# Seven-product tiles: a buffer of its own for the third weight piece, a norm spread over twelve tiles, and one more tile by seven products

## The chip, the cores and the metric

The kernel runs on one core of a Trainium2 chip. The core has a matrix engine (PE, whose weight loads the profile lists as PEld), a vector engine (DVE, called VectorE in words), a scalar engine (ACT, ScalarE), a general engine (POOL, GpSimd) and a queue engine (SP) that issues most of the transfers between device memory and the core's own memory. The metric is the time of one execution on the device in microseconds (us). A profile is of one such execution; its span runs from the first to the last instruction.

## The reference

One layer of a streaming encoder is computed for two request groups with the same weights: 1024 frames of a new stream and 32 frames of a running one, 1056 columns in all. The first half of the layer (input projection, three kinds of mixing heads, output projection, norm) isn't touched by the change. The second half is a gated feed-forward layer and the final norm:

```python
x = _layer_norm(ALPHA * x + (1 + g1) * mix, ln1_g, ln1_b)
h = x * (1 + sc2) + sh2
y = (jax.nn.silu(h @ w_gate) * (h @ w_up)) @ w_down
x = _layer_norm(ALPHA * x + (1 + g2) * y, ln2_g, ln2_b)
```

`D_MODEL` is 1024 and `D_FF` is 2816. Everything is in 32-bit floating point.

## The kernel before, in words

**Precision.** Each operand of a large matrix product is split in two: a rounded copy ("hi", made by ScalarE) and the difference to it ("lo", made by VectorE). A product of 128 x 128 weights with a block of columns is then three matmuls, hi by hi, hi by lo and lo by hi (`gemm`, lines 117 to 119). Weights come in through `weights` (lines 105 and 106): a load into a "raw" buffer, a cast into "whi", a subtraction into "wlo". There are three buffers of each kind (`RAW`, `WB`), each of 1056 columns, used in rotation.

**Two column groups.** Group 0 holds 512 columns, group 1 holds 544 (two cuts of 272). The feed-forward layer runs for group 0 first, then for group 1. The 2816 hidden units are 22 tiles of 128, taken in six groups of tiles (`GROUPS`: 3, 3, 4, 4, 4, 4). For each group of tiles, the gate and up products and their activation are made for each tile, and then the down projection (`down`) adds the group's share to the residual `z`. One tile of the next group is made ahead of each down projection.

**Tiles of seven products.** For group 1, the tiles from `SJ` = 4 to 20 are made by `sup`. Gate and up weights, the two halves of the 1024 rows and the two cuts of columns form a product of 2 x 2 blocks by 2 x 2 blocks, and `sup` forms it with seven block products in place of eight, by sums and differences of blocks. Each block product is four 128-row steps of three matmuls over 272 columns, 12 matmuls. A tile in the plain way (`up`) takes 96 matmuls. What `sup` needs beside its own weights:

- **Combined columns.** `sup_operand` makes the sums and differences of the column blocks once, in four steps (k = 0 to 3), into the tiles `T`. Each step loads two blocks from the buffer `dh` in device memory, does four operations on VectorE (lines 1063 to 1066), and splits two results into hi and lo (lines 1068 and 1069). For even k the landing buffers are "w2h" and "w2l", for odd k the two "c" buffers. The steps run among tiles 0, 1 and 2 of group 1.
- **Summed weight blocks.** `sums` prepares, in device memory, the block `dp[j]` for tile j: a copy of one weight block, twice, issued on SP (line 91), and then an accumulating transfer issued on POOL (line 1040). It's called once for each tile, several tiles ahead.
- **Pieces.** For each tile three loads fill raw buffers: `raw[0]` with 1024 columns of `w_gu`, `raw[1]` with the 1024 columns of `dp[j]`, `raw[2]` with 512 columns of `w_gu`. From `raw[0]` comes w1 (lines 1087 and 1088); then two additions in place (lines 1093 and 1094), the first of which reads `raw[1]`, turn it into the source of w3. From `raw[1]` comes w4, and from `raw[2]` w2, whose halves have their own buffers "w2h" and "w2l".
- **Order of products.** w1 with the first rows, w1 with the second, w3, w4, w3, w4, w2. Their results are drained by lines 1113 to 1117 and 1124 and 1125, with "uv" and "c" as places for partial results, and lines 1119 to 1128 form the activation.

**Group 0's second norm.** While group 1 runs, the final norm of group 0 is done in pieces by the generator `norm0`: for each of two halves of the columns a step for statistics (with matmuls, line 863, and lines 1167 to 1169) and eight steps, one for each 128 rows. One such step has two VectorE operations (1171, 1187), one ScalarE operation (1189) and, for every second one, a store on SP (1194). Two steps follow each tile of seven products, from tile 4 to tile 12. `issue_after` keeps a step's instructions behind the tile's last activation on the same engine.

**Order.** The order of the instructions on each engine and queue is fixed when the kernel is built, by a planner that works with its own estimates of durations; the program text gives the dependencies and the preference. On the chip each engine then runs its list in order. Names in the profile follow buffers: `wo_ah` and `wo_al` are the columns' hi and lo, `lna_ah` and `lna_al` in group 1's tiles are the combined columns `T`, `mlstm_z` is the residual of group 0, `start_dp` is the summed weight block, and "sup_g" and "sup_u" are the two sets of accumulators that the products use in turn.

In the profile tile 3 of group 1 runs from 1050 to 1062 us, the first down projection from 1062 to 1080, tiles 4 to 6 from 1080 to 1113, tiles 7 to 10 from 1132 to 1180, tiles 11 to 14 from 1204 to 1251, tiles 15 to 18 from about 1276 to 1318.

Of the kernel before, what the change touches and what calls it, by code (L numbers as in the profile page):

```python
# [7 lines left out]
F32 = mybir.dt.float32  # L8
# [7 lines left out]
P = 128  # L16
# [29 lines left out]
RAW = 3  # L46
WB = 3
FF = 22
SJ = 4
TS = 1  # L50
ALPHA = 2.0 ** 0.25
LN_EPS = 1e-5
# [13 lines left out]
def f(ap):  # L66
    return ap.bitcast(F32)


class Kernel:  # L70
# [10 lines left out]
    def t(self, pool, shape, dt=F32, tag=None, bufs=None):  # L81
        self.n += 1
        kw = {} if bufs is None else {"bufs": bufs}
        return pool.tile(shape, dt, tag=tag, name=f"{self.phase}_{tag}_{self.n}", **kw)
# [945 lines left out]
    def sums(self):  # L1030
# [5 lines left out]
        if i < FF:  # L1036
            with self.tc.issue_after(self.lastload.ins):
                self.store(self.dp[i], blocks(i)[:, 2:3].to_broadcast([P, 2, 512]))
        if SJ <= i - 1 < FF:
            self.nc.gpsimd.dma_start(self.dp[i - 1], blocks(i - 1)[:, 0:4:3], accum_op=ALU.add)  # L1040

    def sup_operand(self, ks):

        nc = self.nc
        tt = nc.vector.tensor_tensor
        if not self.T:
            self.T = [[self.t(self.ph, [P, 2176], F32R, f"{x}{i}", 1).rearrange("p (k n) -> p k n", k=4)
                       for x in ("ah", "al")] for i in (0, 256)]
        a, b = slice(0, 272), slice(272, 544)
        def load(k):  # L1050
            self.phase = "sup"
            x, y = ((self.t(self.px, [P, 544], F32, "c", 2) for _ in range(2)) if k % 2 else
                    (f(self.t(self.px, [P, 544], F32R, z, 1)) for z in ("w2h", "w2l")))
            self.load(x, self.dh[:, k])
            self.load(y, self.dh[:, k + 4])
            return x, y

        loaded = {k: load(k) for k in ks[:2]}
        yield
        for k in ks:  # L1060
            self.phase = "sup"
            x, y = loaded.pop(k)
            tt(y[:, b], y[:, b], x[:, b], ALU.subtract)
            tt(x[:, b], x[:, a], x[:, b], ALU.subtract)
            tt(x[:, a], y[:, b], x[:, a], ALU.add)
            tt(y[:, a], x[:, a], y[:, a], ALU.subtract)
            for z, (h, l) in zip((x, y), self.T):
                nc.scalar.copy(h[:, k], z)
                tt(l[:, k], z, f(h[:, k]), ALU.subtract)
            if k + 2 in ks:  # L1070
                loaded[k + 2] = load(k + 2)
            yield

    def sup(self, j, act, pool):
        self.phase = "sup"
        nc = self.nc
        tt = nc.vector.tensor_tensor
        hh, hl, T = self.hh[1], self.hl[1], self.T
        ah, al = act[j] = [self.t(pool, [P, GN[1]], F32R, x, 5) for x in ("acth", "actl")]
        raw = [self.t(self.wp, [P, 1056], F32, "raw", RAW)[:, :n] for n in (1024, 1024, 512)]  # L1080
        self.load(raw[0], self.d["w_gu"][j][:, :1024])
        self.load(raw[1], self.dp[j].rearrange("p b n -> p (b n)"))
        self.load(raw[2], self.d["w_gu"][j][:, 1536:])
        lo, hi = slice(0, 512), slice(512, 1024)

        def split(h, l, x):
            nc.scalar.copy(h, x)  # L1087
            tt(l, x, f(h), ALU.subtract)  # L1088
            return [(h[:, k * P:k * P + P], l[:, k * P:k * P + P]) for k in range(x.shape[1] // P)]

        big = lambda x: split(*(self.t(self.wp, [P, 1056], F32R, y, WB)[:, :1024] for y in ("whi", "wlo")), x)
        w1 = big(raw[0])
        tt(raw[0][:, lo], raw[0][:, lo], raw[1][:, hi], ALU.add)
        tt(raw[0][:, hi], raw[0][:, hi], raw[0][:, lo], ALU.add)
        w3 = big(raw[0])
        w4 = big(raw[1])
        w2 = split(*(self.t(self.px, [P, 544], F32R, x, 1)[:, :512] for x in ("w2h", "w2l")), raw[2])
        own = lambda t, k0: (lambda k: hh[t][:, k0 + k], lambda k: hl[t][:, k0 + k])
        com = lambda i: tuple(lambda k, t=t: t[:, k, 272 * (i % 2):272 * (i % 2) + 272] for t in T[i // 2])
        n = [0]  # L1100

        def prod(w, x):
            n[0] += 1
            ps = self.t((self.pg, self.pu)[n[0] % 2], [P, 512], F32, self.utag[n[0] % 2])[:, :272]
            self.gemm(ps, w, slice(0, P), *x)
            return ps

        a, b = slice(0, 272), slice(272, 544)
        u1 = self.t(self.p2, [P, 272], F32, "tmp", 4)
        x = self.t(self.p2, [P, 544], F32, "sil", 2)  # L1110
        uv = self.t(self.px, [P, 544], F32, "uv", 1)
        c = self.t(self.px, [P, 544], F32, "c", 2)
        nc.scalar.copy(u1, prod(w1[:4], own(0, 0)))
        tt(x[:, a], prod(w1[4:], own(0, 4)), u1, ALU.add)
        tt(uv[:, a], u1, prod(w3[:4], com(0)), ALU.subtract)
        tt(uv[:, b], prod(w4[4:], com(1)), uv[:, a], ALU.add)  # L1116
        tt(x[:, b], prod(w3[4:], own(272, 4)), uv[:, b], ALU.add)
        s = self.t(self.p2, [P, 544], F32, "sil", 2)
        nc.scalar.activation(s, x, AF.Exp, scale=-1.0)
        nc.scalar.activation(s, s, AF.Ln, bias=self.one)  # L1120
        nc.scalar.activation(s, s, AF.Exp, scale=-1.0)
        tt(s, x, s, ALU.mult)
        two = lambda y: y.rearrange("p (t n) -> p t n", t=2)
        tt(two(c), prod(w4[:4], com(3)).unsqueeze(1).to_broadcast([P, 2, 272]), two(uv), ALU.add)
        tt(c[:, a], prod(w2, com(2)), c[:, a], ALU.add)
        nc.vector.scalar_tensor_tensor(c, c, -1.0, s, ALU.mult, ALU.mult)
        nc.scalar.copy(ah, c)
        self.lastact = tt(al, c, f(ah), ALU.subtract)
# [78 lines left out]
    def run(self):  # L1207
# [14 lines left out]
        self.dh = t([P, KT, GN[1]], "dh")  # L1222
        self.dp = {j: t([P, 2, 512], f"dp{j}") for j in range(SJ, FF)}
        self.T = []
        self.scq = ()
        self.nsum = SJ
        self.dmix = [t([P, KT, GN[c]], f"dmix{c}") for c in range(2)]
# [18 lines left out]
        w2, w3 = d["w_in"], d["w_in_f"]  # L1246
# [154 lines left out]
        def norm0():  # L1401
            for a, b in LN[0]:
                yield from self.ln2(0, self.st0, a, b, "aaaaaaaa")

        norm0 = norm0()
        for g, (j0, nj) in enumerate(GROUPS):
            for j in range(j0 + (g > 0), min(j0 + nj + (g < last), FF - TS)):
                if self.nsum <= FF:
                    self.sums()
                if j >= SJ:  # L1410
                    self.sup(j, act, pa)
                    with tc.issue_after(self.lastact.ins):
                        next(norm0, None)
                        next(norm0, None)
                    continue
                for i, _ in enumerate(self.up(1, j, act, pa, MM[1])):
                    if 0 < 2 * j + i // 2 < 5 and i % 2:
                        with tc.issue_after(self.lastact.ins):
                            next(operand, None)
            if g < last:  # L1420
                st = self.ln_begin(nc.gpsimd, sum=False) if g == last - 1 else None
                self.down(1, g, act, MM[1], st)
        st.update(pivot=False, sum=True, order=(4, 5, 6, 7, 0, 1, 2, 3))

        n = nj * 256
# [123 lines left out]
```

## Time and profile before

| | us |
|---|---|
| time, median of 3 runs | 1418.04 |
| lowest and highest of them | 1415.65 and 1418.85 |
| the profiled execution | 1418.36 |
| its span | 1416.6 |
| granted clock of the matrix engine, mean over the span | 0.990 |

A row of the profile's table of groups gives line, engine, operation, names (out <- in), shape and count, then busy time and the mean duration of one in ns, then the idle time of the engine just before them and what ended it. A row of the timeline gives start and duration in us. An "x2" behind a row of the timeline means that consecutive instructions of one kind are merged, and the duration covers them all. Matmuls overlap: the records show 0.29 us for one of 272 columns, while the next one starts 0.125 us later.

### The profile page before, as it was taken

The page shows a single profiled execution, that of the slowest core. Times are in us where ns is not written, and L with a number is a line of the kernel's source. Part 1 is how long each engine was busy: PE and PEld are TensorE (multiplying, and loading weights), DVE is VectorE, ACT ScalarE, POOL GpSimd, SP SyncE. Part 2 cuts the span into 40 slices and gives each one's busy share as a digit, 9 for nine tenths or more (in the row PEclk, how much of TensorE's full clock was granted, in tenths as well). Part 3 has the DMA queues.
Part 4 walks back from the last instruction along what each step waited for, and adds up shares of the span by engine and source line. Part 5 has one row for each costly group of instructions (what it writes and reads, how often), then busy time and mean ns, then how long its engine had stood idle before and what let it go on. Part 6 is the DMA issues. An engine that isn't in the chain of part 4 may idle for free.

```text
span 1416.6 us, 28810 instructions
## 1 busy us (share of the span) xinstructions
PE 1364.1 (96%) x10945; PEld 1312.5 (93%) x10945; DVE 1041.1 (73%) x2363; ACT 657.7 (46%) x1395; POOL 255.8 (18%) x298
## 2 busy tenths in 40 slices
PE   7999999999999899999999999999999999999996
PEld 4799988999889789999999999999999999999996
DVE  5548645678679678687777765678977988878777
ACT  3313234444446464555555453335663454535354
POOL 0103200043157400000000000364610000000331
PEclk9999999999999999999999999999999999999999
DMA  9664578575754765344334422654586567542321
GB/s 359 246 216 132 172 224 238 174 229 157 224 185 147 185 206 173 99 142 148 111 112 146 90 98 86 179 172 128 177 214 182 159 176 202 155 135 92 118 98 64
DMA packets 135698, 231.97 MB, mean 164 GB/s; under 512 B 22516, under 2 KB 79484, under 8 KB 135560
## 3 DMA queue, kind: packets, MB, share of 16 engines
q1 hardware_dynamic: 130520, 220.56, 49.2%
q0 software_dynamic: 4896, 9.44, 4.4%
q8 instruction: 86, 1.41, 0.4%
q14 instruction: 52, 0.43, 0.1%
q10 hardware_dynamic: 144, 0.14, 0.0%
HBM read 196.19 MB, written 52.76 MB: 176 GB/s over the span
## 4 chain that ended last, share of the span: by engine, by line
PE 76%; DVE 9%; DMA 8%; ACT 3%; issue 2%; SPq 1%; POOL 1%; DVEq 0%; ACTq 0%; POOLq 0%
PE up_g L118 6%; PE up_g L119 5%; PE up_g L117 5%; PE dn_g L117 4%; PE dn_g L118 4%; PE dn_g L119 4%; PE tm_g L282 3%; PE tm_g L283 3%; PE tm_g L284 3%; PE fm_g L117 2%; PE fm_g L119 2%; PE fm_g L118 2%; PE fox_t L732 2%; PE wo_g L117 2%; PE wo_g L118 2%
## 5 line engine op out<-in xcount | busy, mean ns | idle before, releaser
L117 PE MATMUL up_g<-wo_ah,up_whi 128*128 128x256 f32 (+1 forms) x720 | 205.4, 286 | 3.9 <-ACT lna_tmp L964 3.3
L118 PE MATMUL up_g<-wo_al,up_whi 128*128 128x256 f32 (+1 forms) x720 | 207.4, 288 | 0.6 <-DVE wo_al L969 0.6
L119 PE MATMUL up_g<-wo_ah,up_wlo 128*128 128x256 f32 (+1 forms) x720 | 205.9, 286 | 0.0
L117 PEld LDWEIGHTS up_g<-wo_ah,up_whi 128*128 128x128 f32 x720 | 136.6, 190 | 5.4 <-ACT wo_ah L968 3.5
L118 PEld LDWEIGHTS up_g<-wo_al,up_whi 128*128 128x128 f32 x720 | 136.8, 190 | 1.6 <-DVE wo_al L969 0.8
L119 PEld LDWEIGHTS up_g<-wo_ah,up_wlo 128*128 128x128 f32 x720 | 136.8, 190 | 0.4 <-DVE up_wlo L106 0.2
L117 PE MATMUL fm_g<-start_h1h,fm_whi 128*128 128x256 f32 (+2 forms) x344 | 102.1, 302 | 8.4 <-DVE fm_qkl L367 3.6
L283 PE MATMUL tm_g<-tm_wlo,start_h1h 128*128 128x256 f32 (+1 forms) x384 | 110.1, 287 | 0.0
L284 PE MATMUL tm_g<-tm_whi,start_h1l 128*128 128x256 f32 (+1 forms) x384 | 109.8, 287 | 0.0
L282 PE MATMUL tm_g<-tm_whi,start_h1h 128*128 128x256 f32 (+1 forms) x384 | 109.2, 286 | 0.2 <-ACT tm_mixs L633 0.2
L117 PE MATMUL dn_g<-up_acth,dn_whi 128*128 128x256 f32 (+1 forms) x352 | 102.4, 291 | 0.2 <-DVE sup_uv L1116 0.2
L118 PE MATMUL fm_g<-start_h1l,fm_whi 128*128 128x256 f32 (+2 forms) x344 | 101.7, 296 | 0.0
L119 PE MATMUL fm_g<-start_h1h,fm_wlo 128*128 128x256 f32 (+2 forms) x344 | 101.1, 295 | 0.0
L118 PE MATMUL dn_g<-up_actl,dn_whi 128*128 128x256 f32 (+1 forms) x352 | 100.5, 286 | 0.0
L119 PE MATMUL dn_g<-up_acth,dn_wlo 128*128 128x256 f32 (+1 forms) x352 | 100.4, 285 | 0.0
L1087 ACT CAST sup_whi<-sup_raw 128x1024 fp32r<-128x1024 f32 x51 | 52.7, 1047 | 80.7 <-PE dn_u L118 28.1
L735 ACT CAST fox_pth<-fox_t 128x256 fp32r<-128x256 f32 (+3 forms) x144 | 51.1, 373 | 67.5 <-PE fox_t L732 63.0
L117 PEld LDWEIGHTS fm_g<-start_h1h,fm_whi 128*128 128x128 f32 x344 | 65.4, 192 | 14.0 <-DVE fm_qkl L367 4.3
L106 DVE TENSOR_TENSOR up_wlo<-up_raw,up_whi 128x1024 fp32r<-128x1024 f32 x52 | 66.2, 1273 | 16.5 <-ACT up_whi L105 15.7
L1088 DVE TENSOR_TENSOR sup_wlo<-sup_raw,sup_whi 128x1024 fp32r<-128x1024 f32 x51 | 63.1, 1244 | 17.0 <-ACT sup_whi L1087 17.0
L105 ACT CAST up_whi<-up_raw 128x1024 fp32r<-128x1024 f32 x52 | 54.5, 1047 | 45.2 <-PE up_g L118 19.7
L736 DVE TENSOR_TENSOR fox_ptl<-fox_t,fox_pth 128x256 fp32r<-128x256 f32 (+3 forms) x144 | 58.0, 417 | 23.7 <-ACT fox_pth L735 22.4
(575 smaller groups left out, 4676.9 us busy)
## 6 DMA issues: line engine op xcount, KB each, us to landing
up_raw<-w_gu SPq DMA_DIRECT2D x52, 512.0 KB
dn_raw<-w_dn SPq DMA_DIRECT2D x28, 512.0 KB
ada_late<-w_ada SPq DMA_DIRECT2D x24, 512.0 KB
wo_raw<-w_o SPq DMA_DIRECT2D x24, 512.0 KB
sup_raw<-w_gu SPq DMA_DIRECT2D x19, 512.0 KB
start_dp<-w_gu SPq DMA_DIRECT2D x18, 512.0 KB
start_dp<-w_gu POOLq DMA_DIRECT2D x18, 512.0 KB, 7.6
sup_raw<-start_dp SPq DMA_DIRECT2D x17, 512.0 KB
```

The lines of the kernel that those rows point to most:

```text
L105: nc.scalar.copy(hi[:, :w], raw[:, :w])
L106: (eng or nc.vector).tensor_tensor(lo[:, :w], raw[:, :w], f(hi[:, :w]), ALU.subtract)
L117: nc.tensor.matmul(ps, hi, xh(k), start=start and k == 0, stop=False)
L118: nc.tensor.matmul(ps, hi, xl(k), start=False, stop=False)
L119: nc.tensor.matmul(ps, lo, xh(k), start=False, stop=stop and k == n - 1)
L282: nc.tensor.matmul(ps[:, :ncol], xh, hi, start=k == 0, stop=False)
L283: nc.tensor.matmul(ps[:, :ncol], xh, lo, start=False, stop=False)
L284: nc.tensor.matmul(ps[:, :ncol], xl, hi, start=False, stop=k == 7)
L735: nc.scalar.copy(ph[:, lo:nq], ps[:, lo:nq])
L736: nc.vector.tensor_tensor(pl[:, lo:nq], ps[:, lo:nq], f(ph[:, lo:nq]), ALU.subtract)
L1087: nc.scalar.copy(h, x)
L1088: tt(l, x, f(h), ALU.subtract)
```

## The change

Three edits, all in the part where group 1's feed-forward layer runs. `SJ` goes from 4 to 3: tile 3 is made by `sup`, and the sums of weight blocks begin with tile 3. The third piece of each tile gets a buffer "w2" of its own in the pool `px` and leaves the rotation of raw buffers; to make room there, "c" has one buffer in place of two, and the loads of `sup_operand` for odd k use "c" and "uv". The steps of `norm0` no longer go two to a tile: a list gives 1, 1, 2, 2, 2, 1 steps, twice, to the twelve tiles 3 to 14.

```diff
-SJ = 4
+SJ = 3
...
-            x, y = ((self.t(self.px, [P, 544], F32, "c", 2) for _ in range(2)) if k % 2 else
+            x, y = ((self.t(self.px, [P, 544], F32, z, 1) for z in ("c", "uv")) if k % 2 else
                     (f(self.t(self.px, [P, 544], F32R, z, 1)) for z in ("w2h", "w2l")))
...
-        raw = [self.t(self.wp, [P, 1056], F32, "raw", RAW)[:, :n] for n in (1024, 1024, 512)]
+        raw = [self.t(self.wp, [P, 1056], F32, "raw", RAW)[:, :1024] for _ in range(2)]
+        raw.append(self.t(self.px, [P, 544], F32, "w2", 1)[:, :512])
         self.load(raw[0], self.d["w_gu"][j][:, :1024])
         self.load(raw[1], self.dp[j].rearrange("p b n -> p (b n)"))
         self.load(raw[2], self.d["w_gu"][j][:, 1536:])
...
         uv = self.t(self.px, [P, 544], F32, "uv", 1)
-        c = self.t(self.px, [P, 544], F32, "c", 2)
+        c = self.t(self.px, [P, 544], F32, "c", 1)
...
         norm0 = norm0()
+        turns = [1, 1, 2, 2, 2, 1] * 2
...
                     with tc.issue_after(self.lastact.ins):
-                        next(norm0, None)
-                        next(norm0, None)
+                        for _ in range(turns.pop(0) if turns else 0):
+                            next(norm0, None)
                     continue
```

## The prediction, made before the changed kernel was run

> **What bounds the kernel now.** I read the page first, then the waits of the matrix engine in the last third, then a table of windows over the stage that the change touches, then the chain of waits inside it.
>
> ```profile
> span 1416.6 us, 28810 instructions
> PE 1364.1 (96%) x10945; PEld 1312.5 (93%) x10945; DVE 1041.1 (73%) x2363; ACT 657.7 (46%) x1395; POOL 255.8 (18%) x298
> ```
>
> PE is busy for 96% of the span, so a gain must come from fewer matmuls or from the few places where PE stands still. The waits of PE from 1030 us to the end (what it waited for: total us, times, longest) are few:
>
> ```profile
> PE sup_u L117 <- ACT sup_whi L1087: 5.6, 2, 2.9
> PE sup_u L119 <- DVE sup_wlo L1088: 0.7, 1, 0.7
> ```
>
> All of it lies in the tiles of seven products ("sup" names), where a weight piece wasn't split in time: 6.3 us. The table of windows (start:end, length, busy us and instructions of PE, PEld, DVE, ACT, POOL, granted clock, DMA share, GB/s) shows what they cost in all. The first three rows are tiles 7 to 10, tiles 11 to 14, and tiles 15 to 18.
>
> ```profile
> 1132.60:1175.00 42.40, 38.76 (x291) 38.04 (x291) 35.51 (x61) 23.66 (x37) 2.07 (x2) 0.96 0.65 177
> 1204.00:1250.00 46.00, 43.23 (x328) 42.63 (x327) 36.16 (x60) 23.30 (x34) 2.07 (x2) 0.96 0.59 166
> 1275.50:1318.00 42.50, 42.50 (x340) 42.50 (x340) 36.18 (x56) 24.37 (x34) 0.00 (x0) 1.00 0.35 118
> 1170.90:1174.40 3.50, 3.49 (x16) 3.50 (x17) 3.29 (x4) 2.37 (x3) 0.00 (x0) 0.53 0.79 211
> 1242.30:1245.70 3.40, 3.40 (x17) 3.40 (x18) 3.40 (x5) 2.45 (x3) 0.00 (x0) 0.57 0.71 223
> ```
>
> Tiles 15 to 18 never wait: 340 matmuls in 42.50 us, 0.125 us each. By that rate the first two windows lose 42.40 - 291 x 0.125 = 6.0 us and 46.00 - 328 x 0.125 = 5.0 us, **11.0 us together**. 6.3 us of it is standing still. The last two rows show most of the rest: right after each long wait the granted clock is 0.53 and 0.57 for 3.4 us, in which 16 and 17 matmuls run instead of 28 and 27; that is 1.5 + 1.3 us.
>
> Why the pieces are late is in the chain of waits (start us, us, what), here from tile 8 to tile 10:
>
> ```profile
> 1134.65 3.80 DMA sup_raw<-start_dp
> ...
> 1144.18 7.49 DMA sup_raw<-start_dp
> ...
> 1155.61 1.14 DVE sup_wlo L1088
> ...
> 1156.77 5.82 DMA sup_raw<-w_gu
> ```
>
> The path runs load, adds, split, load: a load starts the moment a split frees a buffer. Three raw buffers serve three pieces of each tile, so every piece of the next tile waits for a piece of this one. From 1144.18 to 1156.77 the loop takes 12.6 us, while a tile of 84 matmuls takes 84 x 0.125 = 10.5. SP's queue shows the same:
>
> ```profile
> 1142.42 0.33 SPq L87 DMA_DIRECT2D sup_raw<-w_gu  x1
> 1144.18 0.33 SPq L87 DMA_DIRECT2D sup_raw<-start_dp  x1
> 1145.13 0.33 SPq L87 DMA_DIRECT2D sup_raw<-w_gu  x1
> 1145.51 0.92 SPq L91 DMA_DIRECT2D start_dp<-w_gu  x1
> 1153.81 0.39 SPq L1194 DMA_DIRECT2D o_yT<-mlstm_z  x1
> 1156.77 0.33 SPq L87 DMA_DIRECT2D sup_raw<-w_gu  x1
> ```
>
> The first three are tile 9's pieces. Tile 10's first piece goes out only at 1156.77 and lands 5.82 later, at 1162.6, with tile 10's first product due about a microsecond after.
>
> **The change part by part.**
>
> *Tile 3 by seven products.* It ran as 2 x 2 x 8 x 3 = 96 matmuls and will run as 84. 12 x 0.125 = **-1.5 us** on PE. It adds work elsewhere: 256 KB more loaded, one more summed weight block (a store on SP, an accumulating DMA on POOL), and more VectorE work. The neighbours:
>
> ```profile
> 1025.02 1.06 POOL L1040 DMA_DIRECT2D start_dp<-w_gu  x1 [1.82 <-DMA start_dp<-w_gu]
> 1029.04 2.39 SPq L87 DMA_DIRECT2D up_raw<-w_gu  x2
> 1034.23 0.33 SPq L87 DMA_DIRECT2D sup_w2h<-start_dh  x1
> start_dp<-w_gu POOLq DMA_DIRECT2D x18, 512.0 KB, 7.6
> ```
>
> All sums move one place, so tile 3's takes POOL's place at 1025.02 and lands about 7.6 later (the median), at 1032.6. Tile 3's load of it stands where the second load of 1029.04 ended (1031.4), so SP may stand for about 1.2 us; behind it is a load that went out at 1034.23 anyway. Cost 0.
>
> The operands of tile 3 are the closer race. Its matmuls start at 1049.96 and the third product, the first that reads the combined operands, is due 24 matmuls later, at 1053.0:
>
> ```profile
> 1049.96 0.29 PE L117 MATMUL up_g<-wo_ah,up_whi 128*128 128x272 f32 x1
> 1047.03 1.05 ACT L105 CAST up_whi<-up_raw 128x1024 fp32r<-128x1024 f32 x1 [0.76 <-PE up_g L118]
> 1048.24 1.22 DVE L106 TENSOR_TENSOR up_wlo<-up_raw,up_whi 128x1024 fp32r<-128x1024 f32 x1
> 1050.37 0.43 DVE L1019 TENSOR_TENSOR up_sil<-up_g,up_sil 128x272 f32<-128x272 f32 x1
> 1050.72 0.71 DVE L1069 TENSOR_TENSOR lna_al<-sup_c,lna_ah 128x544 fp32r<-128x544 f32 x1
> 1050.00:1062.00 12.00, 12.00 (x98) 12.00 (x98) 5.72 (x11) 5.52 (x11) 1.22 (x2) 1.00 0.63 164
> 1062.00:1080.00 18.00, 18.00 (x146) 18.00 (x145) 14.51 (x31) 4.61 (x6) 1.03 (x1) 1.00 0.75 192
> ```
>
> The last operand is made at 1051.43; two adds of 0.68 each (L1093, L1094; the row of L1093 is below) put it at 52.8. The third piece of split weight (w3) can take the cast at 1047.03; the fourth needs one more cast and one more subtraction of 1.22 after 1050, due at 1054.5. So it fits with about 0.2 us to spare on VectorE, which is idle for 6.3 us of the next 12. Bounds: 0, or everything in a row on VectorE (1.22 + 1.36 + 1.24 + 1.24, two subtractions of the last operand at 0.71, three closing operations of the tile before at about 0.44, from 1048.24) until 1056.0, which is 3.0 late, plus the 1.5 of slow clock that followed the long waits: 4.5. I take the value near the rows, **+0.5**.
>
> *The third piece's own buffer.* Two of the three ring buffers are now used per tile, so tile 10's first piece waits for tile 8's fourth-weight split (free at 1144.18, by the load that took the buffer then) and not for tile 9's; behind tile 9's third piece and one store on SP it goes at about 1146.5 instead of 1156.77. The summed piece of tile 9 goes after w3's split of tile 8 (1142.4) instead of 1144.18. The rest of the loop is load 7.49 at worst, two adds, cast, subtraction:
>
> ```profile
> L1093 DVE TENSOR_TENSOR sup_raw<-sup_raw,sup_raw 128x512 f32<-128x512 f32 x17 | 11.6, 683 | 1.6 <-DMA sup_raw<-start_dp 1.6
> L1087 ACT CAST sup_whi<-sup_raw 128x1024 fp32r<-128x1024 f32 x51 | 52.7, 1047 | 80.7 <-PE dn_u L118 28.1
> L1088 DVE TENSOR_TENSOR sup_wlo<-sup_raw,sup_whi 128x1024 fp32r<-128x1024 f32 x51 | 63.1, 1244 | 17.0 <-ACT sup_whi L1087 17.0
> ```
>
> 7.5 + 1.4 + 1.05 + 1.2 = 11.2 with the slowest load and 7.5 with the fastest (3.80), against 10.5 on PE and with a tile more of lead. The waits in tile 10 go, and so does the one in tile 14, whose first piece came the same way. **-11.0 us**; bounds 0 (VectorE or ScalarE are the limit, below) and -11.0. The new buffer's load waits for the split of the third piece before it (SP order puts a sum's store and the next first piece behind it); 1145.13 shows that it waited for just that split already. Cost 0; if it slips, the piece behind it still has 10 us of lead.
>
> *One buffer for c, uv used for loading.* c is written and last read on VectorE, the next tile's write follows in its order; uv is first written by tile 3's third product, after the operand step that reads it (1051.43). Cost 0; bound 0.7, the one wait on VectorE of that length above.
>
> *The norm over twelve tiles.* The same 18 steps, each with two VectorE operations, one on ScalarE, and a store on SP for every second one. Before tile 10's late split, the second half's statistics and a step stood in the way; they move by one tile. In tiles 11 to 13 two steps per tile stay. Steps now reach tile 14 and touch nothing that tiles 15 to 20 wait for (36.18 of 42.50 on VectorE there, and no wait). Moved stores of 0.39 each sit between loads on SP as before: 0.
>
> *What is left.* Short waits of the 0.74 kind will come up somewhere in eleven reshuffled tiles: I allow **+1.0**, between 0 and 2.1 (three of 0.7).
>
> Sum: -1.5 + 0.5 - 11.0 + 1.0 = -11.0. The profiled execution took 1418.36 us (span 1416.6 and 1.8 around it), the median is 1418.04: 1418.36 - 11.0 = 1407.4 there, **1407.0** beside the median. Its own range is 1404.5 to 1410.5.
>
> [...]
>
> **The rivals.**
>
> *Tile 3 takes more.* VectorE is behind at tile 3, a long wait with its slow clock: 4.5 instead of 0.5, 1411.0. For it: 14.51 of 18.00 on VectorE right after. Against: 6.3 us idle just before that.
>
> *One of the two long waits stays*, tile 14's, where norm steps aren't thinned: 5.0 less gained, 1412.0. For it: a norm step's activation stood ahead of the late cast, as the rows show. Against: by the reckoning for tile 10 its first piece, too, comes about a tile sooner.
>
> ```profile
> 1240.13 0.60 ACT L1189 ACTIVATE mlstm_z<-mlstm_z,start_colp 128x256 f32<-128x256 f32 x1
> 1240.63 0.64 ACT L1121 ACTIVATE sup_sil<-sup_sil 128x544 f32<-128x544 f32 x1
> 1241.18 1.98 ACT L1087 CAST sup_whi<-sup_raw 128x1024 fp32r<-128x1024 f32 x2
> ```
>
> *Slow clock without waits.* If the 2.8 us at half clock came from something other than the idle time before, they stay: 1409.8. It is within the forecast's own range.
>
> *The change doesn't do what it says*: the loads aren't issued earlier, because in SP's fixed order they stand behind one that waits, or because the order of casts is what binds. Then only the 1.5 and tile 3's 0.5 count, with +1.0 left out: 1417.0.
>
> *Slower: VectorE is the bound of the tiles, not the ring.* Place: tiles 3 and 4 and the down projection between. Tiles 7 to 10 kept it busy 35.51 of 42.40. If it is full, earlier loads give nothing (0 of 11.0), and one more such tile gives two more waits like those seen: 4.5 in tile 3 and 5.0 in tile 4. 1418.0 - 1.5 + 9.5 = 1426.0. It decides from new waits over 1.5 + 2.8 = 4.3 us. Against: tiles 15 to 18 hold 36.18 of 42.50 and lose nothing.
>
> **How the numbers follow.** Forecast with its own range 0.55 (the slow clock's case, 0.03, inside); tile 3 takes more 0.12; one long wait stays 0.12; no earlier loads 0.12; slower 0.09. Within 0.2% means 1415.2 to 1420.9, about what a measurement of this kernel can tell from no change. So faster 0.55 + 0.12 + 0.12 = 0.79, same 0.12, slower 0.09. The range runs from 1404.5 (every term at its best gives 1418.04 - 12.5 = 1405.5, and 1.0 of the spread of the runs shown, 1415.65 to 1418.85) to 1418.0, which takes in every case but the slower one.
>
> **What would show it.** Right: no wait of PE on L1087 between 1120 and 1250, granted clock 1.00 there, 84 matmuls in tile 3, first pieces issued a tile ahead on SP. Wrong in tile 3: a wait on L1069, L1088 or L1093's followers near 1053. Wrong in the ring: "sup_whi <- DMA sup_raw" still on the chain with a load that starts as a split ends. Wrong on VectorE: PE waits on L1088 with the raw piece long landed.

## The result, and the profile after

| | before | after |
|---|---|---|
| time, median of 5 runs (us) | 1417.29 | 1405.29 |
| lowest and highest of them (us) | 1415.65 and 1418.85 | 1404.46 and 1406.04 |
| the profiled execution (us) | 1418.36 | 1406.04 |
| its span (us) | 1416.6 | 1404.3 |

The change makes the kernel faster: the ratio of the times is 0.9916, with a 95% interval of 0.9904 to 0.9927. The medians differ by 12.0 us, the two spans by 12.3.

First the head of the page of the changed kernel, the same two lines as before:

```profile
span 1404.3 us, 28827 instructions
PE 1360.3 (97%) x10933; PEld 1310.1 (93%) x10933; DVE 1042.7 (74%) x2370; ACT 657.6 (47%) x1394; POOL 258.2 (18%) x299
```

There are 12 matmuls fewer, tile 3's, and yet PE is busy for only 3.8 us less, while the span is 12.3 us shorter. So most of what went was time in which PE stood still or ran at half clock (in the kernel before, the granted clock was 0.50 for 3.41 us behind each of the two long waits; last section). Next the waits of PE from 1030 us to the end in the changed kernel (what it waited for: total us, times, longest):

```profile
PE up_u L119 <- DVE up_wlo L106: 0.4, 1, 0.4
PE lnb_t L863 <- DVE sup_qs L853: 0.2, 1, 0.2
PE lnb_t L863 <- POOL sup_zs L851: 0.2, 1, 0.2
```

The 6.3 us of waits for the casts and subtractions of the seven-product tiles are gone (in the changed program those lines are 1088 and 1089). The table of windows of the changed kernel follows, with the columns of the prediction's (start:end, length, busy us and instructions of PE, PEld, DVE, ACT, POOL, granted clock, DMA share, GB/s). Its rows are tile 3, the first down projection, tiles 7 to 10, and tiles 11 to 14:

```profile
1050.80:1062.00 11.20, 11.20 (x89) 11.14 (x88) 9.43 (x17) 6.87 (x12) 1.03 (x1) 1.00 0.96 274
1062.00:1080.30 18.30, 18.30 (x146) 18.25 (x146) 16.38 (x36) 5.49 (x10) 2.05 (x2) 1.00 0.90 217
1130.50:1173.00 42.50, 42.50 (x340) 42.45 (x339) 36.75 (x60) 24.64 (x37) 1.03 (x1) 1.00 0.59 169
1197.10:1239.40 42.30, 42.30 (x339) 42.30 (x338) 37.11 (x62) 24.59 (x35) 1.03 (x1) 1.00 0.53 151
```

Tiles 7 to 14 now run as tiles 15 to 18 did before: PE without a gap, 0.125 us per matmul, the clock at 1.00. VectorE works more than before in the same windows (36.75 of 42.50, against 35.51 of 42.40), and nothing waits for it. SP's queue in the changed kernel shows what was behind the waits:

```profile
1140.59 0.32 SPq L87 DMA_DIRECT2D sup_raw<-start_dp  x1
1142.35 0.33 SPq L87 DMA_DIRECT2D sup_raw<-w_gu  x1
1143.30 0.33 SPq L87 DMA_DIRECT2D sup_w<-w_gu  x1
1143.69 0.55 SPq L91 DMA_DIRECT2D start_dp<-w_gu  x1
1150.04 0.40 SPq L1195 DMA_DIRECT2D o_yT<-mlstm_z  x1
1153.38 0.33 SPq L87 DMA_DIRECT2D sup_raw<-start_dp  x1
```

These are tile 9's summed piece, tile 10's first piece, tile 9's third piece (now in `sup_w`), a sum's store, a store of the norm, and tile 10's summed piece. Tile 10's first piece is issued at 1142.35, ahead of tile 9's third. The first matmul that needs it starts 20.2 us later:

```profile
1162.55 0.29 PE L117 MATMUL sup_u<-wo_ah,sup_whi 128*128 128x272 f32 x1
```

Before, the same matmul started at 1163.77, 7.0 us after the issue at 1156.77.

**Where the 12.3 us lie.** To compare kernels by stage I use a point that all of them pass at the same place of the work: the last statistics matmul of group 1's first norm, ahead of its feed-forward layer. Its rows, before and after (durations in ns, then the first and last start in us):

```profile
L863 PE MATMUL lna_t<-wo_qs,start_onesm x2: 392/392/392, 990.1 to 990.3; 128*128 128x272 f32 x2
```

```profile
L863 PE MATMUL lna_t<-wo_qs,start_onesm x2: 392/392/392, 991.0 to 991.2; 128*128 128x272 f32 x2
```

From there to the end it was 1416.6 - 990.3 = 426.3 us and is 1404.3 - 991.2 = 413.1: the stage is 13.2 us shorter, and 0.9 came back ahead of it. I call this length "the stage" below.

### The profile page after: what moved, and what is told of

The parts are those of the page before. It is cut to its first block, busy times and chain, and to the rows that moved or that the text cites. A ratio compares the mean times of both kernels' runs of the same rounds, so it can differ in the third digit from the quotient of the medians.

```text
span 1404.3 us, 28827 instructions
## 1 busy us (share of the span) xinstructions
PE 1360.3 (97%) x10933; PEld 1310.1 (93%) x10933; DVE 1042.7 (74%) x2370; ACT 657.6 (47%) x1394; POOL 258.2 (18%) x299
## 4 chain that ended last, share of the span: by engine, by line
PE 81%; DMA 7%; DVE 7%; ACT 2%; issue 1%; SPq 1%; POOL 1%; DVEq 0%; ACTq 0%; POOLq 0%
PE up_g L118 5%; PE up_g L119 5%; PE up_g L117 5%; PE dn_g L117 4%; PE dn_g L118 4%; PE dn_g L119 4%; PE tm_g L282 3%; PE tm_g L283 3%; PE tm_g L284 3%; PE sup_u L119 3%; PE sup_u L117 3%; PE sup_u L118 3%; PE fox_t L732 2%; PE wo_g L118 2%; PE fm_g L117 2%; PE wo_g L117 2%
## 5 line engine op out<-in xcount | busy, mean ns | idle before, releaser
L117 PE MATMUL up_g<-wo_ah,up_whi 128*128 128x256 f32 (+1 forms) x704 | 200.6, 286 | 4.1 <-ACT lna_tmp L964 3.4
L118 PE MATMUL up_g<-wo_al,up_whi 128*128 128x256 f32 (+1 forms) x704 | 202.4, 288 | 0.6 <-DVE wo_al L969 0.6
L119 PE MATMUL up_g<-wo_ah,up_wlo 128*128 128x256 f32 (+1 forms) x704 | 200.9, 286 | 0.0
L117 PEld LDWEIGHTS up_g<-wo_ah,up_whi 128*128 128x128 f32 x704 | 133.3, 190 | 5.6 <-ACT lna_tmp L964 3.5
L118 PEld LDWEIGHTS up_g<-wo_al,up_whi 128*128 128x128 f32 x704 | 133.4, 190 | 1.4 <-DVE wo_al L969 0.8
L119 PEld LDWEIGHTS up_g<-wo_ah,up_wlo 128*128 128x128 f32 x704 | 133.6, 190 | 0.4 <-DVE up_wlo L106 0.2
L1088 ACT CAST sup_whi<-sup_raw 128x1024 fp32r<-128x1024 f32 x54 | 56.0, 1048 | 91.4 <-PE dn_u L118 47.8
L1089 DVE TENSOR_TENSOR sup_wlo<-sup_raw,sup_whi 128x1024 fp32r<-128x1024 f32 x54 | 68.0, 1263 | 10.7 <-ACT sup_whi L1088 10.7
L282 PEld LDWEIGHTS tm_g<-tm_whi,start_h1h 128*128 128x128 f32 x384 | 73.5, 192 | 2.6 <-issue 1.6
L106 DVE TENSOR_TENSOR up_wlo<-up_raw,up_whi 128x1024 fp32r<-128x1024 f32 x50 | 63.3, 1265 | 16.5 <-ACT up_whi L105 16.2
```

Source lines behind the costliest of these rows:

```text
L106: (eng or nc.vector).tensor_tensor(lo[:, :w], raw[:, :w], f(hi[:, :w]), ALU.subtract)
L117: nc.tensor.matmul(ps, hi, xh(k), start=start and k == 0, stop=False)
L118: nc.tensor.matmul(ps, hi, xl(k), start=False, stop=False)
L119: nc.tensor.matmul(ps, lo, xh(k), start=False, stop=stop and k == n - 1)
L282: nc.tensor.matmul(ps[:, :ncol], xh, hi, start=k == 0, stop=False)
```

## The experiments

All ratios are to the kernel before, with 95% intervals. The stage is read from one profile of each kernel. Kernels without waits that should agree in the stage lie up to about 1.3 us apart, so smaller differences say nothing; with the long waits it is more, since a half clock that costs some 1.5 us (28 matmuls less 16, of 0.125 us each) may or may not follow a wait (last section).

| kernel | ratio | stage (us) | PE waits for splits of the seven-product tiles, 1100 us to the end (us) |
|---|---|---|---|
| before | 1 | 426.3 | 6.3 |
| the change | 0.9916 (0.9904 to 0.9927) | 413.1 | 0 |
| tile 3 alone | 0.9972 (0.9954 to 0.9990) | 421.0 | 5.0 |
| own buffer alone | 0.9951 (0.9937 to 0.9965) | 414.1 | 0 |
| spread norm alone | 0.9989 (0.9978 to 1.0001) | 423.0 | 5.6 |
| own buffer and spread norm | 0.9959 (0.9944 to 0.9973) | 414.9 | 0 |
| tile 3 and own buffer | 0.9919 (0.9901 to 0.9938) | 412.3 | 0 |
| tile 3 and spread norm | 0.9989 (0.9975 to 1.0004) | 423.7 | 6.3 |

### One part alone

My theory was that the ring of three raw buffers is the cause, and the own buffer the cure. The rivals were that the norm's steps in the way of the splits are the cause, so that spreading them is the cure, and that the sparing in tile 3 is worth more than its matmuls. The first three runs each make one part of the change alone.

```diff
-SJ = 4
+SJ = 3
```

> Tile 3 by seven products alone, ring and norm as before. Theory (the ring's short supply makes the two long waits): the waits of some 11 us stay somewhere in tiles 4 to 14, only 12 matmuls of 0.125 us go: 1.5 faster, ratio 0.999. Rival (norm crowding makes the waits): the norm now starts a tile earlier with two steps to a tile, so the waits stay too, perhaps moved: 0.999. Rival (any new order of the planner is as good as the change): the waits go here too: 0.991.

The two waits stayed, as this view of its PE waits from 1100 us on shows:

```profile
PE sup_u L117 <- ACT sup_whi L1087: 4.5, 2, 3.0
PE sup_g L117 <- ACT sup_whi L1087: 0.5, 2, 0.4
```

The stage is 5.3 us shorter, of which 1.5 are matmuls, and the ratio, 0.9972, is better than expected. I put the other part down to chance, which no second profile shows: the second long wait was 1.5 us in this execution, and the mean granted clock was 0.991, against 0.990 before. One stretch at half clock less, some 1.5 us by the matmuls in such a stretch (last section), would make up part of it, an estimate. Fewer matmuls alone don't mend the ring.

```diff
-        raw = [self.t(self.wp, [P, 1056], F32, "raw", RAW)[:, :n] for n in (1024, 1024, 512)]
+        raw = [self.t(self.wp, [P, 1056], F32, "raw", RAW)[:, :1024] for _ in range(2)]
+        raw.append(self.t(self.px, [P, 544], F32, "w2", 1)[:, :512])
```

(with the two edits to "c" and "uv" that make room for it)

> The third piece's own buffer alone (with one c buffer and uv as landing place), tiles of seven products from tile 4 and two norm steps to a tile as before. Theory (ring): both long waits go, about 11 us, ratio 0.992, first pieces are issued a tile earlier on SP. Rival (norm crowding): the waits stay, ratio 1.000. A split result, one wait gone and one kept, gives 0.996.

No wait for a split is left, and the stage is 12.2 us shorter. That is the whole gain of the stage but for tile 3's. The time as a whole gained less, 0.9951: ahead of the stage something was lost, which is followed up below.

```diff
+        turns = [1, 1, 2, 2, 2, 1] * 2
...
-                        next(norm0, None)
-                        next(norm0, None)
+                        for _ in range(turns.pop(0) if turns else 0):
+                            next(norm0, None)
```

> The norm spread over twelve tiles (4 to 15) alone, ring and first tile as before. Theory (ring): the waits stay, ratio 0.999 to 1.000, with the chain still running load, split, load. Rival (norm crowding): both long waits go, ratio 0.992.

The waits stayed at 5.6 us:

```profile
PE sup_u L117 <- ACT sup_whi L1087: 5.6, 2, 4.3
```

The time is within 0.2% of the kernel before. Spreading the norm is not the cure.

### One part left out

Leaving out one part of the whole change tests the same from the other side. The change without tile 3:

> The change without tile 3: third piece's own buffer and the spread norm. Theory and the norm rival alike: 11 us gained, ratio 0.9925, 1.5 us slower than the whole change. If tile 3's earlier start were itself what loosened the stage, this would stay near 1.000.

The stage is 414.9, 1.8 us longer than with tile 3 and within scatter of the own buffer alone (414.1). The ratio, 0.9959, misses the 0.9925 expected; as with the own buffer alone, something was lost ahead of the stage. The change without the spread norm:

> The whole change without the spread norm (two steps to a tile, from tile 3). Theory (the own buffer alone removes the waits): no wait of PE on a split between 1040 and 1330, from the last statistics of group 1's first norm to the end about 413 us, as with the whole change, ratio 0.992. Rival (the spread norm is needed once tile 3 is a tile of seven products too): a wait of 1 us or more in tiles 3 to 10, ratio above 0.995.

It is as fast as the whole change (0.9919 against 0.9916), and its stage is 412.3. The spread norm is worth nothing that can be measured here. The change without the own buffer:

> The whole change without the own buffer: tile 3 by seven products and the spread norm, three pieces in the ring. Theory: waits on the split of w3 stay (one of 3 to 4 us and one of 1 to 1.5, as with each of the two alone), some 5 to 7 us of the 11 are left, ratio 0.996. Rival (both easings add up): no wait, ratio 0.992.

All the waits are back, and the ratio is 0.9989, with an interval that holds 1. I had expected that half of the gain would be left (0.996):

```profile
PE sup_u L117 <- ACT sup_whi L1087: 5.8, 2, 3.1
PE sup_u L119 <- DVE sup_wlo L1088: 0.5, 1, 0.5
```

So the own buffer carries the change. In the eight kernels of the table the waits are gone wherever it is in, and there wherever it is out.

### Is the norm a cause at all?

Spreading it did nothing, but that leaves open whether the waits need it. The next kernel is the one before with group 0's second norm left out, so that the rows of the output that belong to group 0 aren't written.

```diff
-                        next(norm0, None)
-                        next(norm0, None)
+                        pass
```

> The kernel before with group 0's second norm left out altogether (its output rows stay unwritten), ring of three for three pieces. Theory (the ring's short supply is the cause, the norm's instructions only add to it): waits on the splits of 1 us or more stay. Rival (VectorE and ScalarE are too full with the norm): no wait at all in tiles 4 to 14, 11 us gained plus about 0.7 for its statistics, ratio 0.991.

The ratio is 0.9933 (0.9911 to 0.9954), the stage 415.4. PE waits for splits in three short waits, 1.4 us together and none longer than 0.5. Neither expectation came true: the theory wanted waits of 1 us or more, the rival none at all.

```profile
PE sup_g L117 <- ACT sup_whi L1087: 0.9, 2, 0.4
PE sup_u L117 <- ACT sup_whi L1087: 0.5, 1, 0.5
```

The loop of load and split is still in its chain of waits, with loads that start as a split ends:

```profile
1137.46 1.06 ACT sup_whi L1087
1138.54 1.24 DVE sup_wlo L1088
1139.79 6.55 DMA sup_raw<-w_gu
1146.42 1.06 ACT sup_whi L1087
```

So the long waits have two causes together: the ring leaves hardly any slack, and the norm's instructions on the same engines use up more than there is. Taking either away ends the long waits. Moving the norm by a tile or two doesn't take it away.

### Lead, or the third piece out of the way?

The own buffer does two things: it gives the other two pieces a third buffer to share, so that they are loaded a tile ahead, and it takes the third piece's split out of the ring. This kernel is the whole change, with one of the three ring buffers held by an unused tile until tile 16. The third piece keeps its own buffer; the lead is taken away.

```diff
+        keep = self.t(self.wp, [P, 1056], F32, "raw", RAW)
+        nc.vector.memset(keep[:, :1], 0.0)
...
+                        if j == 16:
+                            nc.vector.tensor_copy(keep[:, 1:2], keep[:, :1])
```

> The whole change, but one of the three ring buffers is held by an unused tile from group 1's first tile to tile 16, so that the third piece keeps its own buffer and the other two pieces have one buffer each, as the three pieces had before. Theory (the lead that the freed ring buffer gives is what counts): the waits come back, of the size of before or more, since the plain tiles and the down projections have two buffers as well: 10 us or more slower than the whole change, ratio 1.000 or above. Rival (getting the third piece out of the others' way is enough): ratio 0.992 to 0.994.

All of the gain is gone: the ratio is 1.0011 (0.9997 to 1.0025), the stage 422.8, and the waits are back:

```profile
PE sup_u L117 <- ACT sup_whi L1088: 5.4, 2, 3.0
PE sup_u L118 <- DVE lna_al L1069: 0.3, 1, 0.3
```

In SP's queue tile 10's first piece goes out 8.3 us before its first matmul (at 1160.85), against 20.2 with the change and 7.0 before:

```profile
1152.57 0.33 SPq L87 DMA_DIRECT2D sup_raw<-w_gu  x1
```

The lead is what counts, and not that the third piece is out of the way. The down projections in between had two buffers as well, so this kernel doesn't tell the tiles' share of the lead from theirs.

### What the own buffer alone loses ahead of the stage

The own buffer alone reached the stage 6.2 us later than the kernel before (996.5 against 990.3). The statistics of the first norm show where: the first start in these rows is group 0's, the last one group 1's. Before, and with the own buffer alone:

```profile
L863 PE MATMUL lna_t<-wo_qs,start_onesm x8: 378/386/393, 440.0 to 990.3; 128*128 128x256 f32 x4, 128*128 128x272 f32 x4
```

```profile
L863 PE MATMUL lna_t<-wo_qs,start_onesm x8: 378/386/392, 446.3 to 996.5; 128*128 128x256 f32 x4, 128*128 128x272 f32 x4
```

It was 6.3 us behind at 440 us already, where no load of the third piece had been issued. Up to there it has five stretches at half clock (two of them show as a granted clock of 0.51 and 0.52 over the 3.4 us from 205.0 and from 249.1 us; over its whole span the clock was 0.989, against 0.990) where the kernel before has one (0.50 from 143.67 to 147.08); four of them at some 1.5 us each, an estimate from 28 and 16 matmuls of 0.125 us in 3.4 us, are of that size. From 440 to 990 us the two took the same time. But in that part the kernel with the own buffer has waits that the kernel before doesn't have (its waits of PE between 880 and 1030 us), and 6.8 us at half clock in place of 10.2 (before: three stretches of 3.41 us, from 478.2, 874.1 and 880.9) to make up for them:

```profile
PE wo_g L117 <- ACT up_ah L903: 2.3, 1, 2.3
PE wo_g L117 <- DVE up_sil L1019: 0.2, 1, 0.2
```

Both are in the second output projection, and the long one ends at 922.4. SP's queue ahead of the waits:

```profile
905.69 0.39 SPq L87 DMA_DIRECT2D wo_raw<-w_o  x1
906.12 0.64 SPq L87 DMA_DIRECT2D sup_w<-w_gu  x1
906.97 0.62 SPq L91 DMA_DIRECT2D start_dp<-w_gu  x1
907.71 0.60 SPq L87 DMA_DIRECT2D wo_raw<-w_o  x1
```

The second row is the first seven-product tile's third piece, which is split only at 1051.86, some 146 us later. Its buffer is used by nothing else, so nothing held the load back, and the planner put it here. The third row is the store of a summed block, which `sums` ties to the last load; the last load was this one, so the store came along, and the accumulating transfer on POOL after it. The own buffer with the spread norm has the same two transfers there, and a wait of 2.8 us. The following kernel is the own buffer alone with the third load held behind the tile's second:

```diff
+        with self.tc.issue_after(self.lastload.ins):
+            self.load(raw[2], self.d["w_gu"][j][:, 1536:])
```

> The own buffer alone, but its load can only be issued behind the tile's second load, so that neither the first of these loads nor the sum's store that is tied to it goes out some 150 us early, among the loads of the second output projection. Theory (that early traffic costs the 2.3 to 2.8 us of waiting near 921 and now and then a stretch at half clock): the wait near 921 is gone, the stage gains 12 as with the buffer alone, ratio 0.992 in place of 0.995. Rival (the gain is only 7 for another reason, and the 5 in front were chance): ratio 0.995 again.

The wait near 921 us is gone, and so are the two early transfers; the stage is 415.2, and the ratio is 0.9924 (0.9899 to 0.9949) against 0.9951 (0.9937 to 0.9965) without the hold. The intervals overlap, so it is the wait that shows the effect, not the whole time. The same hold put on the whole change:

> The whole change with the third load held behind the second as well. In the whole change only one 256 KB load goes out early, with a wait of 0.3 us near 920 beside it: 0.3 to 0.8 us faster than the whole change, ratio 0.991; if holding it takes away a lead that the tiles need, a wait on w2's split appears and the ratio is above 0.993.

It gains nothing that can be told from scatter: 0.9919 (0.9896 to 0.9942), stage 413.6. In the whole change only the load itself goes early, at 904.47, and beside it lies one wait of 0.3 us, which the held kernel doesn't have:

```profile
PE wo_g L118 <- DVE up_al L904: 0.3, 1, 0.3
```

Why the sum stays behind there I only argue from the program text: with tile 3 by seven products, a down-projection load lies between the third piece and the call of `sums`, so the store is tied to that one.

### One tile further

If tile 3 is worth 1.8 us, tile 2 might be worth as much. This kernel has the held load and `SJ` = 2; the four operand steps move up, so that they lie among tiles 0 and 1.

```diff
-SJ = 4
+SJ = 2
...
-                    if 0 < 2 * j + i // 2 < 5 and i % 2:
+                    if 2 * j + i // 2 < 4 and i % 2:
```

> One tile further: tile 2 by seven products as well (the operand steps half a tile to a tile earlier, all among tiles 0 and 1), with the own buffer, the spread norm (tiles 2 to 13) and the held third load. If PE stays the bound: 12 matmuls or 1.5 us less than with the whole change held, ratio 0.991. If the operands or the two operand splits come too late: a wait of PE on L1069's or L1088's results near the start of tile 2, some 2 to 5 us, ratio 0.993 to 0.995.

It doesn't pay: 0.9938 (0.9918 to 0.9957), stage 416.4. With tile 3 and the held load the stage was 413.6. The wait that was expected on the operands (L1069, L1088) came one step earlier, on the split of plain tile 1's weights. The waits of PE between 1020 and 1050, and the windows ahead of the end of the long one and behind it:

```profile
PE up_u L119 <- DVE up_wlo L106: 1.6, 1, 1.6
PE up_u L117 <- ACT up_whi L105: 0.3, 1, 0.3
```

```profile
1020.00:1027.70 7.70, 5.85 (x45) 5.40 (x43) 7.70 (x19) 6.24 (x14) 1.86 (x3) 1.00 1.03 291
1027.70:1031.10 3.40, 3.37 (x19) 3.37 (x20) 3.40 (x7) 2.94 (x7) 0.00 (x0) 0.67 1.12 265
```

VectorE is busy for all of the 11.10 us, with the operands (lines 1063 to 1069), the running sums of group 0's norm (line 853) and the splits, and the clock behind the wait is 0.67. This is the slower rival's mechanism, one tile further than the change goes.

## Why the prediction was right

**The forecast and its case were right.** The prediction said 1407.0 and -11.0; 1405.29 and -12.0 (spans: -12.3) were measured, near the low end of the forecast's own range. Point by point:

- *Own buffer, -11.0 from tiles 7 to 14.* Right in mechanism and nearly in size. Both windows lose nothing now. The prediction put the long waits down to the ring alone; the kernel without the norm shows that they need both. The stage alone gave -12.2 (own buffer alone); the 1.2 more than the windows hold is about the scatter between two profiles, and isn't located.
- *The issue of the pieces.* Tile 10's first piece was forecast at about 1146.5, "behind tile 9's third piece and one store on SP". It went at 1142.35, ahead of both. The direction was right, and the lead is longer than reckoned; the order on SP was read from the old program, and the planner chose another.
- *Tile 3, -1.5.* Right: -1.8 (own buffer and spread norm against the whole change) and -1.8 (own buffer alone against tile 3 and own buffer), each with the scatter above.
- *Tile 3's operands, +0.5.* **Mis-sized: it was 0, since the prediction timed the wrong operand.** It took the operand that is made last as the one that the third product reads. But each step of `sup_operand` makes two: the first goes into `T[0]`, the second into `T[1]` (line 1067 of the kernel before), and by `com` the third and fourth product read `T[0]`, the sixth and seventh `T[1]`. The last parts of both, and the first matmul of the third product and of the sixth, in the changed kernel:

```profile
1051.55 0.72 DVE L1069 TENSOR_TENSOR lna_al<-sup_c,lna_ah 128x544 fp32r<-128x544 f32 x1
1053.67 0.72 DVE L1069 TENSOR_TENSOR lna_al<-sup_uv,lna_ah 128x544 fp32r<-128x544 f32 x1
```

```profile
1053.84 0.29 PE L117 MATMUL sup_u<-lna_ah,sup_whi 128*128 128x272 f32 x1
...
1058.37 0.29 PE L117 MATMUL sup_g<-lna_ah,sup_whi 128*128 128x272 f32 x1
```

  `T[0]` is whole at 1052.27, 1.6 us ahead of the third product; `T[1]` at 1054.39, 4.0 us ahead of the sixth. The ring of two shows the race lost, and for which operand: its third product waited 0.3 us (the row with L1069 above) until 1053.32. There `T[0]` was whole at 1053.27 and `T[1]` only at 1055.39.
- *What is left, +1.0.* **Mis-sized: 0.** Eleven reshuffled tiles brought no wait of PE; the 0.8 us of waits left after 1030 lie in a plain tile and in the last norm. Without these two terms the sum would have been -12.5, beside -12.3 measured. That this is so close is partly luck: the stage alone gained 13.2, and 0.9 was lost ahead of it, for which the sum has no term.
- *c and uv, the spread norm, the summed block: 0 each.* Right: for the spread norm by the runs with and without it, for the others only in that no wait of PE is put down to them.
- *The one cost that was not in the list* is ahead of the stage: the early load of the third piece. The prediction reckoned the new buffer's load only against the split of the piece before it, and never asked what holds back the first one. In the change a wait of 0.3 us lies beside it; in the two kernels with the own buffer but without tile 3 waits of 2.3 and 2.8.

**The rivals.** Tile 3 taking more, and a long wait staying at tile 14, fell: no such wait is in the trace. That the loads don't go earlier fell with SP's rows. VectorE as the bound fell for this change, with 37.11 of 42.30 us busy and no wait, but holds one tile further on. *Slow clock without waits* fell as well: in tiles 7 to 14 the clock is 1.00 once the waits are gone. The half clock went with the waits: before, it came behind the waits of 2.87 and 2.73 us.

## What to carry to other kernels

When the chain of waits shows the same loop of load, split, load for several tiles, count the buffers against the pieces of a tile: one more place in the ring, even a small one that only takes the smallest piece away, can turn a lead of 7 us into one of 20. What then delays the loop (here a norm on the same engines) is a second cause that need not be touched. A buffer that is free from the start lets its first load go as early as the order allows, so tie it to a later load, and look at what is itself tied to "the last load".

## What the runs showed of the hardware

**Half clock came behind idle times from 1.26 us up, and not always.** I took every single idle time of PE of 0.6 us and more that began at full clock in the profiles before and after the change, from where the record of the clock begins (20.8 and 18.1 us) to 1390 us, and looked whether a stretch at half clock began during it or within 3.41 us behind it, the length of such a stretch:

| idle time of PE (us) | followed by half clock, before | followed by half clock, after |
|---|---|---|
| 2.73 to 3.36 | 4 of 4 | 1 of 1 |
| 1.98 and 2.27 | 0 of 2 | none of this length |
| 1.76 to 1.92 | none of this length | 2 of 3 |
| 1.25 to 1.60 | 0 of 4 | 1 of 4 |
| 0.63 to 1.11 | 0 of 8 | 0 of 5 |

Two of those in the first row are one and the same wait near 475 us, 3.33 us before and 3.36 after. From 1.25 to 2.27 us the length doesn't tell the cases apart: 2.27 us went without, 1.26 us didn't.

**The stretches at half clock lie on a grid of 3.413 us, and in one pair of waits the place on it differs as what followed does.** The clock is recorded in each trace. Ahead of the kernel's end each of the two profiles has six stretches at half clock. All last 3.41 us, and within a profile all of them start whole multiples of 3.413 us apart. Cut along this grid, the kernel before looks like this: the window with the first long wait, the one behind it, and the one behind the second long wait (columns as in the other tables of windows):

```profile
1167.68:1171.09 3.41, 0.54 (x4) 0.32 (x4) 3.38 (x8) 3.41 (x7) 0.00 (x0) 1.00 0.28 85
1171.10:1174.50 3.40, 3.40 (x16) 3.40 (x16) 3.09 (x4) 2.27 (x3) 0.00 (x0) 0.50 0.73 205
1242.78:1246.18 3.40, 3.40 (x17) 3.40 (x17) 3.40 (x6) 1.97 (x3) 0.00 (x0) 0.50 0.74 231
```

The two stretches start 71.68 us apart, 21 times 3.413. Along the grid a pair can be told apart that the lengths can't: early in the kernel, at the same place, PE stood still for 2.27 us before the change and no half clock followed, and for 1.92 us after it and half clock did follow. Before:

```profile
242.66:246.07 3.41, 1.96 (x23) 1.03 (x21) 0.00 (x0) 0.66 (x2) 0.27 (x1) 1.00 0.94 250
246.07:249.48 3.41, 2.59 (x21) 2.57 (x22) 1.73 (x6) 1.04 (x3) 0.00 (x0) 1.00 1.06 328
249.48:252.89 3.41, 3.41 (x28) 3.29 (x27) 2.00 (x9) 0.94 (x3) 0.00 (x0) 1.00 1.00 344
```

After:

```profile
239.92:243.33 3.41, 1.49 (x21) 0.82 (x13) 0.00 (x0) 0.66 (x2) 0.00 (x0) 1.00 0.88 250
243.34:246.74 3.40, 3.40 (x16) 3.30 (x17) 1.82 (x7) 1.15 (x4) 0.00 (x0) 0.50 0.99 311
```

The longer wait lay across a line of the grid, 1.45 us in one window and 0.82 in the next; the shorter one lay in a single window. The window at 249.48 holds 28 matmuls, the one at half clock behind the shorter wait 16, so a halving costs about 12 x 0.125 = 1.5 us on top of the wait.

In the two profiles, from the same start to 1390 us, windows of the grid at full clock in which PE stood still for 2.65 us or more were followed by half clock in 5 of 5 cases, those with 1.40 to 1.92 us in 3 of 7 (before 0 of 3, after 3 of 4). What decides among these stays open; the ends of matmuls in the records are modelled, so the time without one is rough. Of the 780 windows with less, 4 were followed by it, those at 870.71 and 877.54 us before and at 871.38 and 878.21 us after. PE didn't stand still in them; each holds 24 matmuls of 32 columns among its 32 to 36. That these are the reason isn't tested.

The two profiles have no common place for the grid: carried back, a line of it lies 0.3 us behind the first instruction in the profile before and 1.0 us behind it in the one after. In the windows ahead of a half clock PE was busy for part of the time: for 0.54 of 3.41 us in the one with the first long wait, and for 1.49 in the one at 239.92 us after the change.

So in these executions waits of 1.25 to 2.27 us went either way, in the pair above with their place on the grid. This plays ahead of the stage too: the last statistics matmul came between 986.1 and 997.2 us in the profiles of the 13 kernels, and ahead of 440 us the profile after has three stretches at half clock, behind waits of 1.89, 1.92 and 1.26 us, where the one before has one, behind 2.88 us. That is why the stage, measured from a common point, told the kernels apart better than one whole execution did.
